# FFN gate and up: one product of 512 columns for both parts of a block, summed outside TensorE

## The chip, the cores and the metric

The kernel runs on one core of a Trainium2 chip. The metric is the device time of one execution in microseconds (us); the time of a kernel is the median of several executions. The profile is one more execution of the same program, read by the hardware profiler, with its own time.

## The reference

One layer of a decoder trunk for 256 tokens (S) of width 1024 (D), in float32. A mixer of two branches (block-sparse attention and a gated delta rule) comes first; then a feed-forward network (FFN), and then a gate on a per-layer embedding. The change lies in the FFN alone:

```python
f = rms_norm(h, ln_pre_ffn[i])
f = (jax.nn.silu(f @ w_ffn_gate[i]) * (f @ w_ffn_up[i])) @ w_ffn_down[i]
h = h + rms_norm(f, ln_post_ffn[i])
```

`w_ffn_gate` and `w_ffn_up` are 1024 x 2816, `w_ffn_down` is 2816 x 1024.

## The kernel before

Everything is kept transposed: features on the 128 partitions, the 256 tokens along the free dimension. A vector of 1024 features is 8 blocks (KB) of 128 x 256. The hidden width 2816 is 22 tiles (FT) of 128 features.

**Products in three parts.** TensorE multiplies in a type (fp32r) that holds fewer digits than float32. So each operand is split into a high part, rounded by ScalarE (ACT), and a low part, the remainder, computed by VectorE (DVE). A product is then three: high weights with the high part of the block, high weights with its low part, low weights with its high part (`mm3`, lines 242 to 244), all added up in one PSUM area. Each matmul has 256 columns and a load of 128 x 128 weights of its own.

**Weights.** `fetch` (lines 210 to 225) brings a tile of 128 x 1024 weights by DMA into `raw` (4 buffers), ACT writes `whi` (line 223), DVE, or GpSimd (POOL) for a few listed tiles, writes `wlo` (line 224). The gate and up tiles (`fg`, `fu`) share 5 buffers of each part, the down tiles (`fd`) 3. SyncE (SP) issues the DMAs in the order of use, each when a `raw` buffer is free.

**FFN.** The normed activations stand in `fh` and `fl`, eight blocks each. The first two pairs of tiles (t = 0 and 1) go through `four_tiles` (line 891), interleaved with the blocks as they get ready. From t = 2 a loop runs: for t below 22, `pair` makes the gate and the up product of tile t, both into one PSUM bank `pj` of 2 x 256 columns (24 matmuls each); `hidden` (lines 939 to 951) makes the tile's hidden values: multiply by the norm's factor `rs2` (line 941), tanh on ACT (943), the SiLU product (944), times the up half (945), then the split into `fhi` (ACT) and `flo` (DVE), line 263. In the same round `kouter` adds the down product of tile t - 2 into four PSUM banks `oacc` (24 matmuls). Two rounds at the end (t = 22, 23) hold only the down products of the last two tiles. A sum of squares over `oacc` and the rest of the layer follow.

PSUM has three banks for pairs (`bank`, tag "acc"), four for the down sums, one for statistics. `fg` and `fth`, the tiles of `hidden`, come from a pool of 4 buffers (`t1k`).

**Order.** The program is written as one stream; a scheduler sets each engine's order from it, ahead of time, so that each engine then runs a fixed list, in order, with waits on semaphores.

Of the kernel before, what the change touches and what calls it, by code (L numbers as in the profile page):

```python
# [10 lines left out]
F32R = mybir.dt.float32r  # L11
I32 = mybir.dt.int32
AF = mybir.ActivationFunctionType
ALU = mybir.AluOpType

P = 128
S = 256
D = 1024
KB = D // P
# [125 lines left out]
def layer(tc, xT, pT, wpk, wbd, vecs, cst, outT):  # L145
    nc = tc.nc
    ctx = ExitStack()

    def pool(name, bufs, st=ctx, **kw):
        p = st.enter_context(tc.tile_pool(name=name, bufs=bufs, **kw))  # L150
        return p if "space" in kw else Lines(p)
# [20 lines left out]
    def uid(s):  # L172
        count[0] += 1
        return f"{s}_{count[0]}"
# [11 lines left out]
    def t1k(name, dt=F32, pl=tmp, bufs=4):  # L186
        return pl.tile([P, S], dt, tag="t1k", bufs=bufs, name=uid(name))
# [4 lines left out]
    def bank(name):  # L192
        return ps_acc.tile([P, 2, S], F32, tag="acc", name=uid(name))
# [16 lines left out]
    def fetch(parts=1):  # L210
        i = wstate["n"]
        wstate["n"] += 1
        raw = wr.tile([P, D], F32, tag="raw", name=uid("raw_%s%d_%d" % SEQ[i]))
        pl = wstate["late"] if SEQ[i][0] in ("fg", "fu", "pg") and SEQ[i] not in EARLY else wsp
        off = VOFF if SEQ[i][0] == "va" else WOFF
        hi = pl.tile([P, D], F32R, tag="whi", off=off, room=256, name=uid("whi_%s%d_%d" % SEQ[i]))
        lo = pl.tile([P, D], F32R, tag="wlo", off=off, room=256, name=uid("wlo_%s%d_%d" % SEQ[i]))
        n = D // parts
        for c in range(0, D, n):
            cs_ = slice(c, c + n)  # L220
            nc.sync.dma_start(raw[:, cs_], wpk[i][:, cs_])
            with behind(*wstate["gate"]):
                nc.scalar.activation(hi[:, cs_], raw[:, cs_], AF.Copy)  # L223
                (nc.gpsimd if wstate["lo"](i) else nc.vector).tensor_sub(lo[:, cs_], raw[:, cs_], hi[:, cs_].bitcast(F32))  # L224
        wq[SEQ[i]] = (hi, lo)
# [4 lines left out]
    def weight():  # L230

        u = wstate["used"]
        need = max(SEQ.index(w) for w in USE[u:u + wstate["ahead"] + 1])
        while wstate["n"] <= need:
            fetch()
        wstate["used"] += 1
        return wq.pop(USE[u])
# [8 lines left out]
    endmm = [None]  # L246

    def linear(out, w, act, nk=KB, m=P):
        wh, wl = w
        for k in range(nk):  # L250
            mm3(out, wh[:, k * m:(k + 1) * m], wl[:, k * m:(k + 1) * m],
                act[0][:, k], act[1][:, k], k == 0, k == nk - 1)
            if k % 2:
                wv.tick(6 * MM)

    def pair(act):
        ps = bank("pj")
        for j in range(2):
            linear(ps[:, j], weight(), act)
        return ps  # L260

    def split_act(hi, lo, src):
        return nc.scalar.activation(hi, src, AF.Copy), nc.vector.tensor_sub(lo, src, hi.bitcast(F32))  # L263
# [37 lines left out]
    def sq_tiles(pl):  # L301
        return [pl.tile([P, S], F32, tag=f"sqacc{i}", bufs=1, name=uid("sqacc")) for i in range(2)]
# [24 lines left out]
    def stat():  # L327
        return ps_st.tile([P, S], F32, tag="st", name=uid("st"))
# [356 lines left out]
    def v_chunk(w):  # L685
        pv = bank("pv")
        for b in range(2):
            for k in range(KB):
                wh, wl = w[k // 4]
                ws = slice((k % 4) * S, (k % 4 + 1) * S)  # L690
                bs = slice(b * P, (b + 1) * P)
                nc.tensor.matmul(pv[:, b], xg[0][:, k, bs], wh[:, ws], start=k == 0, stop=False)
                nc.tensor.matmul(pv[:, b], xg[0][:, k, bs], wl[:, ws], start=False, stop=False)
                nc.tensor.matmul(pv[:, b], xg[1][:, k, bs], wh[:, ws], start=False, stop=k == KB - 1)
                if k % 2:
                    wv.tick(6 * MM)
        return pv
# [57 lines left out]
    for n, (kind, i) in enumerate(ORDER):  # L755
        if kind in ("kb", "qb"):
            ps = pair(xg)
# [7 lines left out]
        elif kind == "vb":  # L765
            ps = pair(xg)
# [4 lines left out]
        elif kind == "z":  # L771
            if yB[0] is None:
                t = mix.tile([P, 2, H, S], F32R, tag="yB", name="yBt")
                yB[0] = (t[:, 0], t[:, 1])
            ps = pair(xg)
# [5 lines left out]
        elif kind in ("ka", "qa"):  # L781
            ps = pair(xg)
# [5 lines left out]
        elif kind == "va":  # L788
            if yA[0] is None:
                t = mix.tile([P, 2, H, S], F32R, tag="dk", name="yAt")  # L790
                yA[0] = (t[:, 0], t[:, 1])
            w = [weight(), weight()]
            ps = v_chunk(w)
# [22 lines left out]
    for t in range(KB + 2):  # L816
        if t < KB:
            ps = pair(xg)
# [32 lines left out]
    fp = pool("ffn", 1)  # L851
    ft = pool("ffnt", 3)
# [4 lines left out]
    def embed(half):  # L857

        wh, wl = weight()
        got = []  # L860
        for c in range(2):
            ps = bank("pe")
            for j in range(2):
                ms = slice((2 * c + j) * 2 * P, (2 * c + j + 1) * 2 * P)
                for k in range(2):
                    mm3(ps[:, j], wh[:, ms][:, k * P:(k + 1) * P], wl[:, ms][:, k * P:(k + 1) * P],
                        ph[0][:, k], ph[1][:, k], k == 0, k == 1)
            got.append((4 * half + 2 * c, ps))
        return got
# [40 lines left out]
        rs = rsqrt_rep(ft, st, 1.0 / D, eps4, False, last)  # L910
    with behind(lastk):
        eb = embed(0)
    f = (fp.tile([P, KB, S], F32R, name="fh"), fp.tile([P, KB, S], F32R, name="fl"))
    acc = sq_tiles(ft)
    hp = tc.high_priority()
    hp.__enter__()
# [12 lines left out]
    gu, lasthi = four_tiles(f, "gu")  # L929
    wstate["ahead"] = 5  # L930
    st = stat()
    with tc.high_priority():
# [3 lines left out]
        rs2 = rsqrt_rep(ft, st, 1.0 / D, eps1, True, None, gate=True, tanh=True)  # L936
    ea2 = fp.tile([P, S], F32, name="ea2")
    nc.vector.tensor_scalar(ea2, acc[1], 4.0 * EPS, 4.0 * EPS * EPS * D / P, op0=ALU.mult, op1=ALU.add)
    def hidden(ps):
        g_ = t1k("fg", pl=ft)  # L940
        nc.vector.tensor_mul(g_, ps[:, 0], rs2)
        th = t1k("fth", pl=ft)
        nc.scalar.activation(th, g_, AF.Tanh, scale=0.5)
        nc.vector.scalar_tensor_tensor(g_, th, 1.0, g_, op0=ALU.add, op1=ALU.mult)
        nc.vector.tensor_mul(g_, g_, ps[:, 1])
        hi = ft.tile([P, S], F32R, tag="fhi", bufs=4, name=uid("fhi"))
        lo = ft.tile([P, S], F32R, tag="flo", bufs=4, name=uid("flo"))
        last = split_act(hi, lo, g_)
        if wstate["gate"]:
            wstate["gate"] = last  # L950
        return hi, lo

    with tc.high_priority():
        hid = [hidden(gu[0]), hidden(gu[1])]
    db = None
    wstate["ahead"] = 3
    for t in range(2, FT + 2):
        if t < FT:
            hid.append(hidden(pair(f)))
        if t == 5:  # L960
            stf = stat()
            nc.tensor.matmul(stf, ones, ea2, start=True, stop=False)
            embed_sq(0)
        if db is None:
            db = four()
        if t == FT + 1:
            wstate["ahead"] = 5
        lastk = kouter(db, weight(), hid[t - 2][0], hid[t - 2][1], t == 2, t == FT + 1)
        wstate["gate"] = ()
# [19 lines left out]
    pg, _ = four_tiles(h2, "pg")  # L989
# [19 lines left out]
    for m in range(4, KB):  # L1009
        ps = ps_sm.tile([P, 2, S], F32, tag="sm", name=uid("pg"))  # L1010
# [82 lines left out]
```

## Time and profile before

| | |
|---|---|
| time, median of 3 | 607.08 us (605.51 to 610.48) |
| time of the profiled execution | 605.85 us |
| its span, first to last instruction | 604.1 us |
| PE busy | 569.9 us, 94% of the span |
| PE weight loads busy | 552.1 us, 91% |
| DVE busy | 449.4 us, 74% |
| ACT busy | 320.9 us, 53% |
| mean granted TensorE clock | 0.983 of full speed |

The span is read by engine and by stretch. A matmul's own duration contains the way through the array, so the pace of matmuls is read from the distance of their starts. An idle time in brackets is that of the engine just before the instruction, with what ended it.

### The profile page before, as it was taken

How to read it: one execution, taken by the hardware profiler on the slowest of the kernel's cores; microseconds unless marked ns; L12 is line 12 of the kernel's file. 1: busy time of each engine (PE TensorE's matmuls, PEld its weight loads, DVE VectorE, ACT ScalarE, POOL GpSimd, SP SyncE). 2: the span in 40 equal slices, each digit the busy share in tenths (PEclk: the TensorE clock that was granted, in tenths of full speed). 3: DMA queues.
4: the chain of work that ended last, by engine and by line, in shares of the span. 5: the costliest groups of instructions: out<-in, count | busy, mean ns of one | idle time of the engine just before them, and what ended most of it. 6: DMA issues, size and time to landing. Idle time of an engine off the chain costs nothing.

```text
span 604.1 us, 11879 instructions
## 1 busy us (share of the span) xinstructions
PE 569.9 (94%) x4714; PEld 552.1 (91%) x4714; DVE 449.4 (74%) x891; ACT 320.9 (53%) x551; POOL 121.6 (20%) x94
## 2 busy tenths in 40 slices
PE   7798798899798899999999999899999999999997
PEld 6797697799698899999999999889999999999987
DVE  5999999864878975389566667687776666654587
ACT  6744557534357655465545555656554454444643
POOL 4234422412323446100000102420000000001250
PEclk9989988899899999999999999999999999999999
DMA  7655453732235574226666767127875655545502
GB/s 249 223 186 216 128 175 110 222 102 72 69 120 171 138 249 149 96 71 234 206 206 218 234 224 246 58 71 234 272 256 185 205 190 195 192 163 170 175 1 71
DMA packets 40631, 101.95 MB, mean 169 GB/s; under 512 B 9464, under 2 KB 16512, under 8 KB 40448
## 3 DMA queue, kind: packets, MB, share of 16 engines
q1 hardware_dynamic: 40576, 101.20, 51.0%
q8 instruction: 37, 0.61, 0.4%
q14 instruction: 18, 0.15, 0.1%
HBM read 96.70 MB, written 4.48 MB: 168 GB/s over the span
## 4 chain that ended last, share of the span: by engine, by line
PE 65%; DVE 26%; ACT 4%; issue 2%; DMA 1%; POOL 1%; SPq 0%; ACTq 0%; DVEq 0%; POOLq 0%
PE pj L242 11%; PE pj L244 11%; PE pj L243 11%; DVE cy L467 4%; PE oacc L243 4%; PE oacc L242 4%; PE oacc L244 4%; PE pp L244 2%; PE pp L242 2%; PE pp L243 2%; DVE dk L443 2%; PE pg L891 1%; PE pr L590 1%; PE py L596 1%; DVE dk L446 1%
## 5 line engine op out<-in xcount | busy, mean ns | idle before, releaser
L242 PE MATMUL oacc<-fhi,whi_fd 128*128 128x256 f32 x176 | 48.2, 277 | 1.2 <-ACT fhi L263 1.2
L243 PE MATMUL oacc<-flo,whi_fd 128*128 128x256 f32 x176 | 48.7, 278 | 0.3 <-DVE flo L263 0.3
L244 PE MATMUL oacc<-fhi,wlo_fd 128*128 128x256 f32 x176 | 48.5, 276 | 0.0
L243 PE MATMUL pj<-fl,whi_fg 128*128 128x256 f32 x160 | 44.2, 276 | 0.0
L244 PE MATMUL pj<-fh,wlo_fg 128*128 128x256 f32 x160 | 44.2, 276 | 0.0
L242 PE MATMUL pj<-fh,whi_fg 128*128 128x256 f32 x160 | 44.2, 276 | 0.0
L242 PE MATMUL pj<-fh,whi_fu 128*128 128x256 f32 x160 | 44.2, 276 | 0.0
L243 PE MATMUL pj<-fl,whi_fu 128*128 128x256 f32 x160 | 44.2, 276 | 0.0
L244 PE MATMUL pj<-fh,wlo_fu 128*128 128x256 f32 x160 | 44.2, 276 | 0.0
L224 DVE TENSOR_TENSOR wlo_fd<-raw_fd,whi_fd 128x1024 fp32r<-128x1024 f32 x22 | 27.0, 1226 | 22.6 <-ACT whi_fd L223 21.9
L224 POOL TENSOR_TENSOR wlo_pg<-raw_pg,whi_pg 128x1024 fp32r<-128x1024 f32 x4 | 8.2, 2063 | 165.4 <-ACT whi_pg L223 165.4
L223 ACT ACTIVATE whi_fd<-raw_fd 128x1024 fp32r<-128x1024 f32 x22 | 23.3, 1061 | 30.2 <-DMA raw_fd<-wpk 16.3
L223 ACT ACTIVATE whi_fg<-raw_fg 128x1024 fp32r<-128x1024 f32 x22 | 23.3, 1060 | 26.4 <-PE pj L243 19.0
L467 DVE SCALAR_TENSOR_TENSOR cy<-xr,vec,cy 128x254 f32<-128x254 f32 (+2 forms) x72 | 36.6, 547 | 0.9 <-ACT cy L465 0.7
L242 PEld LDWEIGHTS oacc<-fhi,whi_fd 128*128 128x128 f32 x176 | 32.8, 188 | 1.4 <-ACT fhi L263 1.4
L224 DVE TENSOR_TENSOR wlo_fg<-raw_fg,whi_fg 128x1024 fp32r<-128x1024 f32 x21 | 25.7, 1224 | 10.8 <-ACT whi_fg L223 10.8
L223 ACT ACTIVATE whi_fu<-raw_fu 128x1024 fp32r<-128x1024 f32 x22 | 23.3, 1058 | 19.5 <-PE pj L243 13.4
L243 PEld LDWEIGHTS oacc<-flo,whi_fd 128*128 128x128 f32 x176 | 33.0, 188 | 0.5 <-DVE flo L263 0.5
L244 PEld LDWEIGHTS oacc<-fhi,wlo_fd 128*128 128x128 f32 x176 | 33.0, 188 | 0.0
L224 DVE TENSOR_TENSOR wlo_fu<-raw_fu,whi_fu 128x1024 fp32r<-128x1024 f32 x19 | 23.3, 1224 | 12.9 <-ACT whi_fu L223 12.8
L242 PEld LDWEIGHTS pj<-fh,whi_fg 128*128 128x128 f32 x160 | 30.0, 188 | 0.0
L244 PEld LDWEIGHTS pj<-fh,wlo_fu 128*128 128x128 f32 x160 | 30.0, 188 | 0.0
(383 smaller groups left out, 2318.3 us busy)
## 6 DMA issues: line engine op xcount, KB each, us to landing
raw_fg<-wpk SPq DMA_DIRECT2D x22, 512.0 KB, 3.5
raw_fu<-wpk SPq DMA_DIRECT2D x22, 512.0 KB, 4.3
raw_fd<-wpk SPq DMA_DIRECT2D x22, 512.0 KB, 3.4
raw_qb<-wpk SPq DMA_DIRECT2D x8, 512.0 KB, 3.3
raw_ka<-wpk SPq DMA_DIRECT2D x8, 512.0 KB, 3.4
raw_qa<-wpk SPq DMA_DIRECT2D x8, 512.0 KB, 3.7
raw_vb<-wpk SPq DMA_DIRECT2D x8, 512.0 KB, 3.3
raw_va<-wpk SPq DMA_DIRECT2D x8, 512.0 KB, 3.7
```

What stands on the lines that cost most here:

```text
L223: nc.scalar.activation(hi[:, cs_], raw[:, cs_], AF.Copy)
L224: (nc.gpsimd if wstate["lo"](i) else nc.vector).tensor_sub(lo[:, cs_], raw[:, cs_], hi[:, cs_].bitcast(F32))
L242: nc.tensor.matmul(out, wh, xh, start=start, stop=False, **kw)
L243: nc.tensor.matmul(out, wh, xl, start=False, stop=False, **kw)
L244: endmm[0] = nc.tensor.matmul(out, wl, xh, start=False, stop=stop, **kw)
L443: nc.vector.scalar_tensor_tensor(dk[:, h, dst], row[:, j, b * P:(b + 1) * P], gcT[:, b, h:h + 1], mS, op0=ALU.subtract, op1=ALU.max)
L446: nc.vector.scalar_tensor_tensor(dk[:, h, dst], row[:, j, b * P:(b + 1) * P], gcT[:, b, h:h + 1], mB, op0=ALU.subtract, op1=ALU.min)
L467: nc.vector.scalar_tensor_tensor(y[:, j, sh:], xr[:, j, :S - sh], col(w + 3 - sh), y[:, j, sh:], op0=ALU.mult, op1=ALU.add)
L590: nc.tensor.matmul(pr[:, i * P:(i + 1) * P], A[:, h4[i]], Y[:, h4[i]], start=True, stop=True)
L596: nc.tensor.matmul(py[:, i * P:(i + 1) * P], X[:, i], R[:, i], start=True, stop=True)
L891: endmm[0] = nc.tensor.matmul(bk[i // 2][:, i % 2], w[:, k * P:(k + 1) * P], x[:, k], start=start and i % 2 == 0, stop=stop, skip_group_ch ...
```

## The change

`fh` and `fl` become two halves of one tile `fhl`. A new function `wide` makes one product of a weights tile: for each block the high weights meet the high and the low part side by side, 512 columns in one matmul, into a whole PSUM bank `pw` of 2 x 256 columns; the low weights meet the high part, 256 columns, added into the first half. A new function `summed` adds the halves: ACT copies the second half out of PSUM into a tile `fs`, DVE adds the first half to it. `hidden` now takes two operands: for t = 0 and 1 the PSUM areas as before, for t = 2 to 21 two `fs` tiles. A round thus has 16 matmuls per product instead of 24, two PSUM banks instead of one, two more instructions on ACT and two more on DVE.

```diff
-    f = (fp.tile([P, KB, S], F32R, name="fh"), fp.tile([P, KB, S], F32R, name="fl"))
+    fhl = fp.tile([P, 2, KB, S], F32R, name="fhl")
+    f = (fhl[:, 0], fhl[:, 1])
...
-    def hidden(ps):
+    def wide(act):
+
+        wh, wl = weight()
+        ps = bank("pw")
+        for k in range(KB):
+            nc.tensor.matmul(ps, wh[:, k * P:(k + 1) * P], act[:, :, k], start=k == 0, stop=False, skip_group_check=True)
+            endmm[0] = nc.tensor.matmul(ps[:, 0], wl[:, k * P:(k + 1) * P], act[:, 0, k], start=False, stop=k == KB - 1,
+                                        skip_group_check=True)
+        return ps
+
+    def summed(ps):
+        t = t1k("fs", pl=ft)
+        nc.scalar.activation(t, ps[:, 1], AF.Copy)
+        nc.vector.tensor_add(t, t, ps[:, 0])
+        return t
+
+    def hidden(g0, up):
         g_ = t1k("fg", pl=ft)
-        nc.vector.tensor_mul(g_, ps[:, 0], rs2)
+        nc.vector.tensor_mul(g_, g0, rs2)
...
-        nc.vector.tensor_mul(g_, g_, ps[:, 1])
+        nc.vector.tensor_mul(g_, g_, up)
...
-        hid = [hidden(gu[0]), hidden(gu[1])]
+        hid = [hidden(gu[i][:, 0], gu[i][:, 1]) for i in range(2)]
...
-            hid.append(hidden(pair(f)))
+            hid.append(hidden(*[summed(wide(fhl)) for _ in range(2)]))
```

The lines of `hidden` move: 941, 943, 944 and 945 become 958, 960, 961 and 962; the copy and the add of `summed` are lines 952 and 953.

**DVE, one round in the middle of the loop.** The names are those above; numbers behind a name tell buffers apart. Before:

```order
L941 TENSOR_TENSOR fg_5524<-pj_5463,rsr_4910 128x256
L224 TENSOR_TENSOR wlo_fg_0_892_5668<-raw_fg_0_890_5666,whi_fg_0_891_5667 128x1024
L944 SCALAR_TENSOR_TENSOR fg_5524<-fth_5526,fg_5524 128x256
L945 TENSOR_TENSOR fg_5524<-fg_5524,pj_5463 128x256
L224 TENSOR_TENSOR wlo_fd_0_902_5738<-raw_fd_0_900_5736,whi_fd_0_901_5737 128x1024
L263 TENSOR_TENSOR flo_5531<-fg_5524,fhi_5530 128x256
L224 TENSOR_TENSOR wlo_fu_0_895_5698<-raw_fu_0_893_5696,whi_fu_0_894_5697 128x1024
```

Now, the same round:

```order
L953 TENSOR_TENSOR fs_5440<-fs_5440,pw_5423 128x256
L958 TENSOR_TENSOR fg_5469<-fs_5440,rsr_4909 128x256
L224 TENSOR_TENSOR wlo_fg_0_912_5603<-raw_fg_0_910_5601,whi_fg_0_911_5602 128x1024
L953 TENSOR_TENSOR fs_5466<-fs_5466,pw_5449 128x256
L961 SCALAR_TENSOR_TENSOR fg_5469<-fth_5471,fg_5469 128x256
L962 TENSOR_TENSOR fg_5469<-fg_5469,fs_5466 128x256
L224 TENSOR_TENSOR wlo_fd_0_926_5665<-raw_fd_0_924_5663,whi_fd_0_925_5664 128x1024
L263 TENSOR_TENSOR flo_5476<-fg_5469,fhi_5475 128x256
L224 TENSOR_TENSOR wlo_fu_0_917_5629<-raw_fu_0_915_5627,whi_fu_0_916_5628 128x1024
```

One add stands ahead of the multiplication by `rs2`, the other ahead of line 961; the rest keeps its order.

**ACT, where the loop begins**, from the tanh of tiles 0 and 1 on. Before:

```order
L943 ACTIVATE fth_4924<-fg_4922 128x256
L943 ACTIVATE fth_4934<-fg_4932 128x256
L263 ACTIVATE fhi_4928<-fg_4922 128x256
L263 ACTIVATE fhi_4938<-fg_4932 128x256
L223 ACTIVATE whi_fg_0_785_4944<-raw_fg_0_784_4943 128x1024
```

Now:

```order
L960 ACTIVATE fth_4923<-fg_4921 128x256
L960 ACTIVATE fth_4933<-fg_4931 128x256
L952 ACTIVATE fs_4964<-pw_4947 128x256
L263 ACTIVATE fhi_4927<-fg_4921 128x256
L952 ACTIVATE fs_4990<-pw_4973 128x256
L263 ACTIVATE fhi_4937<-fg_4931 128x256
L223 ACTIVATE whi_fg_0_784_4942<-raw_fg_0_783_4941 128x1024
```

A copy for tile 2 stands ahead of each `fhi`.

**ACT, where the last tile's hidden values are made.** Before:

```order
L223 ACTIVATE whi_fd_0_1077_6939<-raw_fd_0_1076_6938 128x1024
L223 ACTIVATE whi_pg_0_1068_6897<-raw_pg_0_1067_6896 128x1024
L223 ACTIVATE whi_pg_0_1074_6933<-raw_pg_0_1073_6932 128x1024
L943 ACTIVATE fth_6970<-fg_6968 128x256
L263 ACTIVATE fhi_6974<-fg_6968 128x256
```

Now:

```order
L223 ACTIVATE whi_fd_0_1135_6762<-raw_fd_0_1134_6761 128x1024
L223 ACTIVATE whi_pg_0_1124_6724<-raw_pg_0_1123_6723 128x1024
L952 ACTIVATE fs_6752<-pw_6735 128x256
L223 ACTIVATE whi_pg_0_1132_6756<-raw_pg_0_1131_6755 128x1024
L952 ACTIVATE fs_6784<-pw_6767 128x256
L960 ACTIVATE fth_6789<-fg_6787 128x256
L263 ACTIVATE fhi_6793<-fg_6787 128x256
```

Both copies stand ahead of the tanh (`pg` are tiles of the stage after the FFN).

## Rows read from the trace of the kernel before

**Rows 1.** The page: busy time of each engine, and the chain that ended last.
```profile
PE 569.9 (94%) x4714; PEld 552.1 (91%) x4714; DVE 449.4 (74%) x891; ACT 320.9 (53%) x551; POOL 121.6 (20%) x94
PE 65%; DVE 26%; ACT 4%; issue 2%; DMA 1%; POOL 1%; SPq 0%; ACTq 0%; DVEq 0%; POOLq 0%
```

**Rows 2.** Windows in the loop: stretch, length, PE, PEld, DVE, ACT, POOL busy, granted clock.
```profile
440.00:480.00 40.00, 40.00 (x356) 40.00 (x355) 27.81 (x38) 19.75 (x26) 0.00 (x0) 1.00 0.65 212
520.00:560.00 40.00, 40.00 (x356) 40.00 (x355) 22.58 (x32) 16.49 (x22) 2.00 (x1) 1.00 0.52 172
```

**Rows 3.** Timeline of PE, one round: start, duration, instruction.
```profile
480.55 0.28 PE L242 MATMUL oacc<-fhi,whi_fd 128*128 128x256 f32 x1
...
483.27 0.28 PE L242 MATMUL pj<-fh,whi_fg 128*128 128x256 f32 x1
...
488.71 0.28 PE L242 MATMUL oacc<-fhi,whi_fd 128*128 128x256 f32 x1
```

**Rows 4.** Timeline of PE in the mixer: float32 products of 512, 256 and 1 columns.
```profile
67.02 1.02 PE L494 MATMUL G<-kq 128*128 128x512 f32 x2
67.88 0.59 PE L496 MATMUL G<-kq 128*128 128x256 f32 x2
68.31 0.50 PE L498 MATMUL G<-cs,qs 128*128 128x1 f32 x4
68.67 0.36 PE L242 MATMUL pj<-xhl,whi_vb 128*128 128x256 f32 x1
```

**Rows 5.** Groups of instructions on DVE and ACT, 407 to 566 us.
```profile
L224 DVE TENSOR_TENSOR wlo_fd<-raw_fd,whi_fd 128x1024 fp32r<-128x1024 f32 x21 | 25.8, 1226 | 22.6 <-ACT whi_fd L223 21.9 <-PE pj L244 0.8
L944 DVE SCALAR_TENSOR_TENSOR fg<-fth,fg 128x256 f32<-128x256 f32 x20 | 9.1, 456 | 1.0 <-ACT fth L943 1.0
L941 DVE TENSOR_TENSOR fg<-pj,rsr 128x256 f32<-128x256 f32 x20 | 8.4, 422 | 8.4 <-PE pj L244 8.3
L223 ACT ACTIVATE whi_fd<-raw_fd 128x1024 fp32r<-128x1024 f32 x21 | 22.3, 1062 | 30.2 <-DMA raw_fd<-wpk 16.3 <-PE oacc L243 11.8 <-PE oacc L244 1.4
L943 ACT ACTIVATE fth<-fg 128x256 f32<-128x256 f32 x20 | 8.0, 401 | 2.5 <-DVE fg L941 2.5
```

**Rows 6.** Timelines of ACT and DVE: three instructions in that round, one reading PSUM.
```profile
480.68 1.06 ACT L223 ACTIVATE whi_fg<-raw_fg 128x1024 fp32r<-128x1024 f32 x1 [1.71 <-PE pj L243]
...
481.78 1.23 DVE L224 TENSOR_TENSOR wlo_fg<-raw_fg,whi_fg 128x1024 fp32r<-128x1024 f32 x1 [0.61 <-ACT whi_fg L223]
...
571.35 0.38 ACT L320 ACTIVATE sq<-oacc 128x256 f32<-128x256 f32 x1
```

**Rows 7.** Timelines of ACT, PE and DVE where the loop begins.
```profile
406.06 0.42 ACT L263 ACTIVATE fhi<-fg 128x256 fp32r<-128x256 f32 x1 [0.64 <-DVE fg L945]
406.53 0.38 PE L242 MATMUL oacc<-fhi,whi_fd 128*128 128x256 f32 x1 [1.23 <-ACT fhi L263]
406.73 0.42 DVE L263 TENSOR_TENSOR flo<-fg,fhi 128x256 fp32r<-128x256 f32 x1
408.25 1.23 DVE L224 TENSOR_TENSOR wlo_fg<-raw_fg,whi_fg 128x1024 fp32r<-128x1024 f32 x1 [0.43 <-ACT whi_fg L223]
409.83 0.28 PE L242 MATMUL pj<-fh,whi_fg 128*128 128x256 f32 x1
```

**Rows 8.** Timelines of ACT, POOL, DVE and PE where the loop ends.
```profile
543.19 1.06 ACT L223 ACTIVATE whi_pg<-raw_pg 128x1024 fp32r<-128x1024 f32 x1 [0.81 <-PE pj L243]
561.47 1.06 ACT L223 ACTIVATE whi_fd<-raw_fd 128x1024 fp32r<-128x1024 f32 x1 [0.89 <-DMA raw_fd<-wpk]
563.56 4.22 POOL L224 TENSOR_TENSOR wlo_pg<-raw_pg,whi_pg 128x1024 fp32r<-128x1024 f32 x2 [17.23 <-ACT whi_pg L223]
564.34 0.40 ACT L943 ACTIVATE fth<-fg 128x256 f32<-128x256 f32 x1
564.77 1.16 DVE L944 SCALAR_TENSOR_TENSOR fg<-fth,fg 128x256 f32<-128x256 f32 x1 [0.64 <-ACT fth L943]
566.87 1.20 DVE L263 TENSOR_TENSOR flo<-fg,fhi 128x256 fp32r<-128x256 f32 x1 [0.48 <-ACT fhi L263]
568.12 0.39 PE L243 MATMUL oacc<-flo,whi_fd 128*128 128x256 f32 x1 [0.26 <-DVE flo L263]
```

## The prediction

> **What bounds the kernel now.** The page comes first: PE is busy 94% of the span and holds 65% of the chain that ended last, DVE 26% of it [rows 1]. Those are averages, so the windows inside the FFN loop come next: in 440 to 480 and in 520 to 560 us PE is busy without a gap and at full clock (granted 1.00, the 2.4 GHz level), while DVE is busy 27.8 and 22.6 us of 40 and ACT 19.8 and 16.5 [rows 2]. So from about 407 us, where the loop gets going, nearly to its end at 568 us nothing but the pace of the matmuls sets the time; a copy or an add on ACT or DVE is beside it as long as it makes nobody late. PE waits at two places only: 1.23 us at the start of the loop, for `fhi` of the first tile [rows 7], and 0.26 us at its end, for `flo` of the last [rows 8].
>
> The pace: a round holds 72 matmuls (24 down, 48 gate and up) and lasts from 480.55 to 488.71 us, 8.16 us, 113.3 ns each [rows 3]. At 2.4 GHz that is 272 cycles for 256 columns: 106.7 ns if a column takes a cycle, and 6.7 ns more. The change leaves the columns as they are (512 + 256 in place of 3 x 256); what it can save on PE is a part of those 6.7 ns.
>
> **What the products give.** Per block, three matmuls become two: 20 tiles x 2 products x 8 blocks = 320 matmuls fewer, each with its load of weights. The first of the 20 rounds ends in PE's wait for `fhi`, which is set by DVE and ACT, not by PE, so its 16 count for nothing; 304 remain. The trace has no fp32r matmul of 512 columns, so its pace is bounded from both sides. If the 6.7 ns are a price of the columns, 512 take 2 x 113.3 = 226.6 ns and nothing is saved. The rows say this is possible: the float32 products of 512 and 256 columns, which the trace shows in two passes each, take 0.86 / 2 = 430 and 0.43 / 2 = 215 ns a pass, in proportion, with next to nothing fixed [rows 4]. The other end is the same 215 ns read differently: a pass of 256 columns that lasts 516 cycles is as long a stream, beside one weight load, as 512 fp32r columns would be, and has only 2 ns on top of 213.3. Then a block takes 215 + 113.3 = 328.3 in place of 340 ns, and 304 x 11.7 ns = 3.5 us go. Between them lies a fixed price for each matmul and its load: 220 + 113.3, 304 x 6.7 ns = 2.0 us. I take 2.0: in the loop every matmul has exactly one load and one start beside it, and these are what the change makes fewer; the float32 passes read a column in two cycles and may hide them. Range 0 to 3.5. That the two halves of the 512 columns lie 8 KB apart in `fhl` has no row; if that costs, it moves toward the end of 0, and past it only if the break costs more than a second matmul does.
>
> The trace's 6.7 ns stand against the Trainium skill, "TensorE: Matmul & The Clock Gate", section "Back-to-back issue gap", which gives a matmul a fixed 2.5 ns beyond its columns; by that the saving would be 304 x 2.5 ns = 0.8 us, and the sum below would be 1.2 us higher. The same page, section "LDWEIGHTS (loading the stationary operand)", prices a load of 128 columns at 128 / 1.2 = 107 ns, by which the load and not the columns could set the pace of 113.3; the four one-column products of [rows 4] with their loads take 0.36 us, 90 ns each, so the rows don't bear that out; by the rule a block would take 213.3 + 113.3 ns, and 304 x 13.3 ns = 4.0 us would go.
>
> **What ACT and DVE get.** Forty copies on ACT, each from PSUM, 128 x 256: 0.38 us in the nearest row that reads PSUM [rows 6], 0.40 for a tanh of that size [rows 5]; 40 x 0.40 = 16 us. Forty adds on DVE with one operand in PSUM, like line 941: 0.42 us [rows 5], 40 x 0.42 = 16.8 us. What hides them is PE's round of 8.16 us, then 8.16 - 16 x 0.0067 = 8.05. DVE's round is three `wlo` of 1.23, line 944 with 0.46 and three of 0.42, 5.4 us in all; with two adds 6.2, or 77% of the round. ACT's is three `whi` of 1.06 and two of 0.40, 4.0; with two copies 4.8, or 60%.
>
> Shares don't show waits, so I walk through a round in the new order, time 0 being the end of the gate product. ACT copies at 0.1 to 0.5 and splits `fg` to 1.6; DVE adds at 0.5 to 0.9, multiplies by `rs2` to 1.3, makes `wlo_fg` to 2.8. The up product ends at 2.65; ACT copies to 3.1, does tanh to 3.5, `whi_fd` to 4.6, `fhi` to 5.0, `whi_fu` to 6.0. DVE adds at 3.15 to 3.6, goes on to 4.45 (two steps), `wlo_fd` from 4.6 to 5.8, `flo` to 6.25, `wlo_fu` to 7.5. The next gate product ends at 8.05, so about one microsecond of a round stays open.
>
> Behind the new waits stand: on ACT, behind the copy of the up half, tanh and the split of the next weights; on DVE, behind its add, the hidden values and three `wlo`. Who waits for those has time. Five buffers hold gate and up tiles: the one split from 480.68 on [rows 6] is freed when the product before ends and is met three rounds on, at 483.27 + 2 x 8.16 = 499.6 by [rows 3], over 16 us after its `wlo` ended at 483.0. A tile's hidden values are needed by the down product two rounds later. The third PSUM bank: the up product of the next round takes the bank of this round's gate product, which is free 0.9 us after that product's end and wanted 8.05 us after, so 7.1 us are open. DMAs carry the same bytes in the same order; a `raw` buffer is freed by `wlo`, which stays as often as before. Cost in the middle of the loop: 0, up to the rival below.
>
> **The two ends of the loop.** At the start ACT had 0.64 us of idle time ahead of `fhi` [rows 7], since it waited for DVE; the copy of 0.40 that now stands there fits in, as the gate product of tile 2 is long over. On DVE the first add stands ahead of `flo`, in the time in which that waited for `fhi`. What is moved is the next split: `wlo_fg` began at 408.25 and was over at 409.48, and PE's product began at 409.83 [rows 7]; with the second copy (0.40) and two adds (0.84) ahead, less the 0.43 that DVE idled there, it ends near 410.3, 0.25 us after the second matmul of that product wants it. PE's new list has a matmul of the up product in between. I put 0.1, range 0 to 0.4.
>
> At the end both copies stand ahead of the last tanh: ACT's tanh at 564.34 [rows 8] becomes 565.14, line 944's successor ends at 566.7 (1.16 us, as long as POOL runs on to 567.8), the product at 567.2, `fhi` at 567.6, `flo` from 567.67 to 568.1 without POOL or 568.9 with it. It ended at 568.07 before, when PE waited for it. So 0 to 0.8 are lost, 1.6 if copies and adds all fall in line (2 x 0.40 + 2 x 0.42). I take 0.4. What PE gains ahead of that is not lost to this chain as a whole: it starts from a split that waits for PE's product at 543 us [rows 8], with most of the gain behind it. What DMA landings hold in it (0.89 us ahead of the last `whi_fd`) moves along with it.
>
> Sum, against the profiled execution: 605.85 - 2.0 + 0.1 + 0.4 = 604.35. The median of the runs is 1.23 us above that execution; so 607.08 - 1.5 = **605.6 us**. The three runs before spread over 605.5 to 610.5, so a change below about 1% (6 us) can't be told from none.
>
> **The rivals.**
> (a) The columns set the pace: no saving, and the ends cost 0.5 us: 607.6; with both ends at their worst (0.4 + 1.6) 609.1. For it stand the proportional float32 rows; against it, that the loads fall by a third.
> (b) A matmul of 512 columns has only the 2 ns on top: 607.08 - 3.5 + 0.5 = 604.1.
> (c) Slower: PE waits for a PSUM bank. DVE idled 2.7 us of a round (8.16 less 5.4), nearly all waiting for ACT's splits and for PE's products [rows 5]. If these waits do not shrink, its round is 6.2 + 2.7 = 8.9 us against PE's 8.05: it falls 0.88 us back each round, has used up the 7.1 us of the bank after 8 rounds, and sets the other 11 of the 19 at 8.9 in place of 8.16 us: + 8.5, less 8 x 0.11 gained before, + 7.6, with the ends 615.2. It decides where DVE's waits in a round stay above 1.8 us. Against it: those waits end with PE or with ACT, which wait for PE's freed buffers (1.71 us ahead of `whi_fg` [rows 6]); that is slack that shrinks when the engine is late.
> (d) The number of columns hardly sets the pace, only the number of matmuls: 304 x 113.3 ns = 34 us less, 573. The float32 passes of 430 against 215 ns speak against it [rows 4]. The section "Back-to-back issue gap" named above has such a rule in the Trainium skill, a sustained 131 ns for 512 columns, by which 304 x 96 ns = 29 us would go; no row here agrees.
>
> **How the numbers follow.** The forecast, 604.5 to 606.9 us with small errors at the ends, has 0.60; (a) 0.19; (b) 0.13; (c) 0.06; (d) 0.02. (a), (b) and the forecast all lie within 1%. The range goes from 602.6 (case (b) with nothing lost at the ends and 1 us for the spread of runs) to 609.6 ((a) at its worst and a little of the spread); outside are (c) and (d) and the spread's rest. Faster by over 1%: (d) and a little of (b), 0.04. Slower by over 1%: (c) and a little of (a), 0.08. The rest, 0.88, is no change that can be told.
>
> **What the profile after would show.** Right: in the loop a 512-column matmul followed by one of 256 at a distance of about 220 ns, the next at 113; a round of about 8.05 us; PE without idle time between the two ends of the loop; DVE near 77% and ACT near 60% there; the last `flo` still the thing PE waits for. (a) shows 227 ns, (b) 215. (c) shows PE idle ahead of line 945 with DVE's line 953 as what ended it. The prediction would be most wrong if a strided moving operand or a shared PSUM bank made the wide matmul slower than two narrow ones, which no row here can exclude.

## The result and the profile after

The changed kernel takes 609.63 us (median of 20 runs), the kernel before 605.90 in the 20 runs beside it: a ratio of 1.0051, 95% interval 1.0034 to 1.0068. It is slower by half a per cent, where 0.25% faster was forecast; the time is also just above the range. The profiled execution took 611.85 us with a span of 610.1 and a mean granted clock of 0.978.

The page of the kernel after, its busy times and its chain, against [rows 1]:

```profile
PE 575.4 (94%) x4394; PEld 543.5 (89%) x4394; DVE 465.2 (76%) x931; ACT 332.3 (54%) x591; POOL 121.0 (20%) x94
PE 64%; DVE 25%; ACT 5%; DMA 2%; issue 2%; POOL 1%; SPq 0%; DVEq 0%; ACTq 0%; POOLq 0%
```

PE has 320 matmuls fewer and is busy 5.5 us longer; weight loads are down by 8.6 us. DVE's and ACT's 40 instructions more add 15.8 and 11.4 us. The chain is as before, mostly PE.

Of the 6.0 us between the two profiled executions, not all lies in the changed stage. The rows that bound it are the first sum of squares ahead of it, the first down product and the sum of squares behind it. Timeline of PE, first of the kernel before:

```profile
381.06 0.67 PE L325 MATMUL st<-sqacc,cs 128*128 128x256 f32 x2 [0.18 <-PE pe L243]
...
571.68 0.70 PE L325 MATMUL st<-sqacc,cs 128*128 128x256 f32 x2
```

Then of the kernel after:

```profile
383.60 0.67 PE L325 MATMUL st<-sqacc,cs 128*128 128x256 f32 x2 [0.18 <-PE pe L243]
...
409.04 0.62 PE L242 MATMUL oacc<-fhi,whi_fd 128*128 128x256 f32 x3 [0.66 <-ACT fhi L263]
...
577.65 0.70 PE L325 MATMUL st<-sqacc,cs 128*128 128x256 f32 x2
```

At 383.60 the execution is already 2.54 us late, with nothing changed so far: in its first 100 us, in the mixer, the granted clock was 0.91, before 0.95. That is not the change's. From there to the first down product it takes 25.44 us, before 25.47 (406.53 by [rows 7]). The loop, from the first down product to the sum of squares behind, takes 577.65 - 409.04 = 168.61 us, before 571.68 - 406.53 = 165.15: **3.46 us more**, which is 0.57% of the time and agrees with the ratio. All that follows is about these 3.46 us.

The windows of the loop after, columns as in [rows 2]:

```profile
440.00:480.00 40.00, 40.00 (x273) 36.82 (x272) 29.64 (x47) 21.97 (x36) 0.00 (x0) 1.00 0.61 203
520.00:560.00 40.00, 40.00 (x268) 36.63 (x267) 27.21 (x43) 19.23 (x31) 2.00 (x1) 1.00 0.52 176
```

PE is still busy without a gap and at full clock. DVE is at 74 and 68%, ACT at 55 and 48%: PE waits for neither of them, nor for a PSUM bank. So the time is in the pace of the matmuls. PE, one round:

```profile
434.75 0.28 PE L242 MATMUL oacc<-fhi,whi_fd 128*128 128x256 f32 x1
...
437.47 0.39 PE L945 MATMUL pw<-fhl,whi_fg 128*128 128x512 f32 x1
437.70 0.28 PE L946 MATMUL pw<-fhl,wlo_fg 128*128 128x256 f32 x1
437.82 0.39 PE L945 MATMUL pw<-fhl,whi_fg 128*128 128x512 f32 x1
...
443.06 0.28 PE L242 MATMUL oacc<-fhi,whi_fd 128*128 128x256 f32 x1
```

The starts are to be compared. The down product takes 437.47 - 434.75 = 2.72 us, as before (483.27 - 480.55, [rows 3]). The round takes 8.31 here, 8.32 in the mean, before 8.16: the gate and up products are 0.16 us longer in a round, 10 ns in each of their 16 blocks. A finer split of a block can't be read from rows rounded to 10 ns: a round lasts the same 8160 ns before, and 8320 after, again and again, so that the rounding falls alike in each round and doesn't average out (some numbers of the expectations below, such as 232 and 118 ns, are such means). By the starts in whole ns that the trace holds, a block before took 113.1 ns (high weights, high part), 113.0 (high, low) and 113.9 (low, high), 340 in all. Now the wide matmul takes 230.5 and the narrow one 119.3, 350 in all. The wide one is 4.4 ns slower than the two that it replaces, and the narrow one beside it 5.4 slower than it was. 19 rounds of 0.16 us are 3.04 of the 3.46 us; the rest is 0.42 at the two ends of the loop.

### The profile page after: what moved, and what is told of

It is laid out like the page before. It is cut to its first block, busy times and chain, and to the rows that moved or that the text cites. A ratio compares the mean times of both kernels' runs of the same rounds, so it can differ in the third digit from the quotient of the medians.

```text
span 610.1 us, 11332 instructions
## 1 busy us (share of the span) xinstructions
PE 575.4 (94%) x4394; PEld 543.5 (89%) x4394; DVE 465.2 (76%) x931; ACT 332.3 (54%) x591; POOL 121.0 (20%) x94
## 4 chain that ended last, share of the span: by engine, by line
PE 64%; DVE 25%; ACT 5%; DMA 2%; issue 2%; POOL 1%; SPq 0%; DVEq 0%; ACTq 0%; POOLq 0%
PE pw L945 10%; PE pj L244 6%; PE pj L242 6%; PE pj L243 6%; PE pw L946 5%; PE oacc L244 4%; PE oacc L243 4%; PE oacc L242 4%; DVE cy L467 4%; PE pp L242 2%; PE pp L244 2%; PE pp L243 2%; DVE dk L443 2%; DMA raw_fd<-wpk 2%; PE pg L891 1%
## 5 line engine op out<-in xcount | busy, mean ns | idle before, releaser
L945 PE MATMUL pw<-fhl,whi_fu 128*128 128x512 f32 x160 | 56.9, 393 | 0.0
L945 PE MATMUL pw<-fhl,whi_fg 128*128 128x512 f32 x160 | 56.9, 392 | 0.0
L946 PE MATMUL pw<-fhl,wlo_fg 128*128 128x256 f32 x160 | 45.2, 282 | 0.0
L946 PE MATMUL pw<-fhl,wlo_fu 128*128 128x256 f32 x160 | 45.1, 282 | 0.0
L945 PEld LDWEIGHTS pw<-fhl,whi_fu 128*128 128x128 f32 x160 | 30.0, 188 | 6.8
L945 PEld LDWEIGHTS pw<-fhl,whi_fg 128*128 128x128 f32 x160 | 30.1, 188 | 5.6
L946 PEld LDWEIGHTS pw<-fhl,wlo_fg 128*128 128x128 f32 x160 | 30.1, 188 | 0.1
L946 PEld LDWEIGHTS pw<-fhl,wlo_fu 128*128 128x128 f32 x160 | 30.0, 188 | 0.0
```

The source lines that it names most:

```text
L945: nc.tensor.matmul(ps, wh[:, k * P:(k + 1) * P], act[:, :, k], start=k == 0, stop=False, skip_group_check=True)
L946: endmm[0] = nc.tensor.matmul(ps[:, 0], wl[:, k * P:(k + 1) * P], act[:, 0, k], start=False, stop=k == KB - 1, skip_group_check=True)
```

## Experiments

The theories of the first runs, as the expectations number them: (1) the two halves of the 512 columns lie 8 KB apart, and the break costs; (2) the wide matmul's own pace is slower, wherever its two halves lie; (3) the new copies and adds, which read PSUM while PE writes it, slow the matmuls. Later expectations split theory 2 by where in it the price might lie, and name each version. A distance is the mean of the distances of starts in the loop, in ns of the trace, unless rows are shown; the granted clock is 1.00 there in every run (412 to 540 us). The time that a run stands beside is that of the kernel before, taken along with it.

**e1: the two parts side by side in SBUF**

```diff
-    fhl = fp.tile([P, 2, KB, S], F32R, name="fhl")
+    fhl = fp.tile([P, KB, 2, S], F32R, name="fhl")
...
-  nc.tensor.matmul(ps, wh[:, k * P:(k + 1) * P], act[:, :, k], ...
+  nc.tensor.matmul(ps, wh[:, k * P:(k + 1) * P], act[:, k], ...
```

> The tile of both parts is laid out block by block (high part of block k, then its low part), so that the 512 columns of a wide matmul are one run of addresses in place of two that lie 8 KB apart; nothing else changes. In the changed kernel a block takes 350 ns (wide matmul 232, narrow one 118), against 340 before. Theory 1 (the break in the moving operand costs): the wide matmul falls to 220 or less, a block to 333 to 340 ns, and the time falls by 3 to 5 us against the changed kernel, to 0.993 to 1.000 of the kernel before. Theory 2 (a long stream of fp32r columns beside a load of other weights costs this, wherever it lies): block 350, time 1.005 of before, as the changed kernel. Theory 3 (the copies and adds, or their reads of PSUM, slow the matmuls): block 350 as well.

Measured: 609.36 against 607.32 us beside it, ratio 1.0024 (0.9997 to 1.0051); wide 230.1 ns, narrow 119.6, round 8.32, loop 168.61 us. PE in this kernel:

```profile
438.26 0.39 PE L945 MATMUL pw<-fhl,whi_fu 128*128 128x512 f32 x1
438.50 0.28 PE L946 MATMUL pw<-fhl,wlo_fu 128*128 128x256 f32 x1
438.62 0.39 PE L945 MATMUL pw<-fhl,whi_fu 128*128 128x512 f32 x1
```

A block of 360 by these rows, which are rounded to 10 ns, and 350 in the mean: 512 adjacent columns are no faster than 256 and 256 with 8 KB between them. Theory 1 falls. The ratio can't be told from that of the change; the loop is the same to 0.01 us.

**e2: the sums stay, the wide matmul is two narrow ones again**

```diff
-  nc.tensor.matmul(ps, wh[:, k * P:(k + 1) * P], act[:, :, k], ...
+  for j in range(2):
+      nc.tensor.matmul(ps[:, j], wh[:, k * P:(k + 1) * P], act[:, j, k], ...
```

> The wide matmul is written as two of 256 columns again, the high part into the first half of the bank and the low part into the second; copies, adds and the two banks a round stay. Theories 1 and 2: three matmuls in 340 ns a block as before, time 0.999 to 1.002 of before (only the end of the loop loses 0.4 us). Theory 3 (copies, adds or PSUM): a block of 347 to 350 ns, time 1.004 to 1.006 of before.

Measured: 608.15 against 607.32 us, ratio 1.0029 (1.0002 to 1.0056); round 8.16, loop 166.91 us. PE in this kernel (a row may hold two matmuls that follow each other):

```profile
437.98 0.39 PE L946 MATMUL pw<-fhl,whi_fu 128*128 128x256 f32 x2
...
438.32 0.39 PE L946 MATMUL pw<-fhl,whi_fu 128*128 128x256 f32 x2
438.54 0.28 PE L948 MATMUL pw<-fhl,wlo_fu 128*128 128x256 f32 x1
438.66 0.28 PE L242 MATMUL oacc<-fhi,whi_fd 128*128 128x256 f32 x1
```

340 ns a block (437.98, 438.32, 438.66), with every copy and every add in place. Theory 3 falls: the round is back at 8.16 and only the width of the matmul was undone. What is left, 1.76 us more than before where 0.4 was expected, lies at the two ends. At the head the second down block starts 0.43 us later after the first than before (9.17 against 8.74) and lasts 3.02 in place of 2.72, 0.73 in all; the rest, about 1.0, is the tail:

```profile
560.11 1.06 ACT L223 ACTIVATE whi_fd<-raw_fd 128x1024 fp32r<-128x1024 f32 x1 [0.58 <-DMA raw_fd<-wpk]
561.06 0.28 PE L242 MATMUL oacc<-fhi,whi_fd 128*128 128x256 f32 x1
562.42 0.42 DVE L955 TENSOR_TENSOR fs<-fs,pw 128x256 f32<-128x256 f32 x1
562.88 1.69 DVE L960 TENSOR_TENSOR fg<-fs,rsr 128x256 f32<-128x256 f32 x1
567.67 0.38 PE L242 MATMUL oacc<-fhi,whi_fd 128*128 128x256 f32 x1 [1.01 <-ACT fhi L263]
```

PE waits 1.01 us for `fhi` of the last tile; before it waited 0.26 for `flo` [rows 8]. The last tile's chain begins behind `whi_fd` and `wlo_fd`, that is behind a DMA, so the first add stands 562.42 - 561.06 = 1.36 us behind the start of the down block. In the changed kernel PE is later at this place, the add stands only 568.45 - 567.87 = 0.58 behind the same block, and the wait is 0.23: the 0.78 us of difference is exactly what PE waits less. So the sums cost 1.76 us where PE keeps its pace of before; in the changed kernel the slower rounds cover a part of it.

**e3: the wide matmul stays, the sums are left out** (the hidden values are made from the first half alone)

```diff
-    hid.append(hidden(*[summed(wide(fhl)) for _ in range(2)]))
+    hid.append(hidden(*[wide(fhl)[:, 0] for _ in range(2)]))
```

> The wide matmuls stay, but nothing copies or adds the second half: the hidden values are made from the first half alone, so the product of the high weights with the low part is left out of the result. Theories 1 and 2: block 350 ns, round 8.31 us as in the changed kernel. Theory 3: block 333 to 340 ns.

Measured: 608.72 us in one execution; round 8.32, wide 230.2 ns, narrow 119.5, loop 167.51 us; PE doesn't wait at the tail. Without one copy or add the matmuls are as slow as with them. This is the counterpart of e2: the width by itself costs 2.36 us of loop (3.04 by the pace, less 0.68 at the ends), the sums by themselves 1.76, both together 3.46. On top of the width, then, the sums cost 1.10 us.

**e4: all eight wide matmuls first, then all eight narrow ones**

```diff
   for k in range(KB):
       nc.tensor.matmul(ps, wh[:, k * P:(k + 1) * P], act[:, :, k], ...
+  for k in range(KB):
       endmm[0] = nc.tensor.matmul(ps[:, 0], wl[:, k * P:(k + 1) * P], act[:, 0, k], ...
```

> In each product the eight wide matmuls come first, then the eight narrow ones, so that a wide matmul is followed by a load of the next high weights and not of low ones. Theory 1 (break): the wide matmul keeps 232 ns or near it, a block stays 345 to 352 ns. Theory 2 in the form that the change between high and low weights costs: wide 218 to 225, narrow 107 to 113, block 330 to 340. Theory 3: block 350.

Measured: 608.47 us in one execution; round 8.29 to 8.30. PE in this kernel:

```profile
438.81 1.09 PE L947 MATMUL pw<-fhl,wlo_fu 128*128 128x256 f32 x8
439.74 0.28 PE L242 MATMUL oacc<-fhi,whi_fd 128*128 128x256 f32 x1
...
442.46 2.02 PE L945 MATMUL pw<-fhl,whi_fg 128*128 128x512 f32 x8
444.32 0.86 PE L947 MATMUL pw<-fhl,wlo_fg 128*128 128x256 f32 x6
```

Eight wide matmuls take 444.32 - 442.46 = 1.86 us, 232.5 ns each; eight narrow ones 439.74 - 438.81 = 0.93, 116 each. The wide one is as slow among its like as beside a narrow one, and the narrow ones are slower than the 113.3 of before even among their like: it isn't the alternation.

**e5: another place of the gate and up weights in their buffers**, at an offset of 0, and of 24, in place of 88

```diff
-  off = VOFF if SEQ[i][0] == "va" else WOFF
+  off = VOFF if SEQ[i][0] == "va" else 0 if SEQ[i][0] in ("fg", "fu") else WOFF
```

> The changed kernel with the gate and up weights (both parts) at offset 0 within their buffers in place of 88 bytes; the offset was chosen with matmuls of 256 columns. Theory 2a (the stream of fp32r columns and the load of weights beside it get in each other's way in the on-chip memory, depending on their addresses): the wide matmul moves by at least 3 ns from 232, in either direction, and with it the round of 8.32 us by at least 0.05 us. Theory 2b (512 columns of fp32r take 232 ns by themselves): 232 ns, round 8.30 to 8.34 us.

> The same with offset 24 (88 less 64). Theory 2a: if the addresses count modulo 64 bytes, as offset 88 (232 ns, 8.32 us a round); if they count in larger units, another value. Theory 2b: 232 ns, round 8.30 to 8.34 us.

Measured, one execution each, beside 612.04 us: offset 0, 613.42 us, round 8.39, wide 236 ns, narrow 117; offset 24, 607.99 us, round 8.28 to 8.29, wide 233, narrow 114. So a block takes 353, 347 or 350 ns at offsets of 0, 24 and 88. At offset 0 the wide matmul moves by more than the 3 ns of theory 2a: the place of the weights does move the pace, by a few ns. But none of the three comes down to the 340 of before.

**e6: half the load beside the wide matmul** (the narrow matmul has 64 columns of weights: half the rows of its part of the sum are left out)

```diff
-  endmm[0] = nc.tensor.matmul(ps[:, 0], wl[:, k * P:(k + 1) * P], act[:, 0, k], ...
+  endmm[0] = nc.tensor.matmul(ps[:64, 0], wl[:, k * P:k * P + 64], act[:, 0, k], ...
```

> The narrow matmul takes only the first 64 columns of the low weights, so that the load that runs beside the wide matmul has half its columns; the low weights' part of the other 64 features is left out of the result. Theory 2a: the 19 ns that the wide matmul takes beyond 213 shrink by half, to 222 to 224 ns, and a round gets 0.14 us shorter or more. Theory 2b: the wide matmul stays at 232 ns, the round at 8.32 us; at most the narrow one changes.

Measured: 610.17 us in one execution, beside 612.04; round 8.29 to 8.30. PE in this kernel:

```profile
446.66 0.39 PE L945 MATMUL pw<-fhl,whi_fg 128*128 128x512 f32 x1
446.89 0.28 PE L946 MATMUL pw<-fhl,wlo_fg 128*64 128x256 f32 x1
447.01 0.39 PE L945 MATMUL pw<-fhl,whi_fg 128*128 128x512 f32 x1
```

Wide 230.3 ns, as with the full load to within 1 ns: what is loaded while the wide matmul runs doesn't set its pace. The load that runs beside the narrow one, of the next high weights, is still a full one. The Trainium skill, "TensorE: Matmul & The Clock Gate", section "LDWEIGHTS (loading the stationary operand)", makes a load's price proportional to its columns, an estimated 107 ns for 128; the load halved here, hidden either way, shows that such a price isn't in these 230 ns.

**e7: the wide matmul reads only the upper two bytes of each number** (as bf16; the lower digits of both operands are left out), the narrow one as before

```diff
-  nc.tensor.matmul(ps, wh[:, k * P:(k + 1) * P], act[:, :, k], ...
+  nc.tensor.matmul(ps, wh.bitcast(mybir.dt.bfloat16)[:, 2 * k * P + 1:2 * (k + 1) * P:2],
+                   act[:, :, k].bitcast(mybir.dt.bfloat16)[:, :, 1::2], ...
```

> The wide matmul reads only the upper two bytes of each number, weights and block (as bf16 at a step of 4 bytes); the lower digits are left out of the result. Same columns, same addresses, same loads in number. Theory 2a: with half the bytes the wide matmul falls to 213 to 220 ns, the round to 8.1 us or less. Theory 2b in the form that the type fp32r costs: the same. Theory 2c (any matmul of 512 columns beside a 128-column load takes 232 ns): 232 ns, round 8.32 us.

Measured: 611.73 us in one execution, beside 612.04; round 8.51 to 8.54. PE in this kernel:

```profile
446.76 0.40 PE L945 MATMUL pw<-fhl,whi_fu 128*128 128x512 bf16 x1
446.80 0.48 PE L947 MATMUL pw<-fhl,wlo_fu 128*128 128x256 f32 x1
447.12 0.40 PE L945 MATMUL pw<-fhl,whi_fu 128*128 128x512 bf16 x1
```

Starts of 41 and 320 ns apart, 361 a block: where types alternate, the records no longer part one matmul from the next, and the change of type has a price of its own. This run tells nothing about bytes; e9 was made for that.

**e8: fewer columns in the wide matmul** (448, 384, 320 of the 512, on top of e1 and e3: the rest of the low part and the sums are left out)

```diff
-  nc.tensor.matmul(ps, wh[:, k * P:(k + 1) * P], act[:, k], ...
+  nc.tensor.matmul(ps.rearrange("p a b -> p (a b)")[:, :448], wh[:, k * P:(k + 1) * P],
+                   act[:, k].rearrange("p a b -> p (a b)")[:, :448], ...
```

> The wide matmul of the block-by-block layout takes 448 columns: the 256 of the high part and the first 192 of the low part; what the other columns would give is left out, and so are the copies and adds (the hidden values are made from the first half, as in the run without sums, which kept the pace). So only the number of columns changes; with 512 the wide matmul takes 231.5 ns. Theory 2d (fp32r columns come at a price each, somewhat over a cycle, with a small credit for each matmul; a line through 113 ns at 256 and 231.5 at 512): 202 ns. Theory 2e (a fixed 6.7 ns up to some number of columns, and a further fixed price past it): 193 ns if the price is not due yet, 205 if it is.

> The same with 384 columns (256 of the high part, 128 of the low part). Theory 2d: 172 ns. Theory 2e: 167 ns if the further price is not due yet, 178 if it is.

> The same with 320 columns (256 of the high part, 64 of the low part). Theory 2d: 143 ns. Theory 2e: 140 ns if the further price is not due yet, 152 if it is.

Measured, beside 606.31 us:

| columns | time, us | round, us | wide, ns | ns per column | narrow, ns |
|---|---|---|---|---|---|
| 512 (e1, with sums) | 609.36 (beside 607.32) | 8.32 | 230.1 | 0.449 | 119.6 |
| 448 | 600.52 | 7.86 to 7.92 | 202.8 | 0.453 | 116.9 |
| 384 | 591.02 | 7.41 | 174.7 | 0.455 | 118.3 |
| 320 | 582.11 | 6.97 | 146.1 | 0.457 | 118.0 |

PE in the kernels of 448, 384 and 320 columns, in this order:

```profile
442.70 0.36 PE L945 MATMUL pw<-fhl,whi_fg 128*128 128x448 f32 x1
442.90 0.28 PE L947 MATMUL pw<-fhl,wlo_fg 128*128 128x256 f32 x1
```

```profile
442.67 0.34 PE L945 MATMUL pw<-fhl,whi_fu 128*128 128x384 f32 x1
442.84 0.28 PE L947 MATMUL pw<-fhl,wlo_fu 128*128 128x256 f32 x1
```

```profile
444.29 0.31 PE L945 MATMUL pw<-fhl,whi_fg 128*128 128x320 f32 x1
444.44 0.28 PE L947 MATMUL pw<-fhl,wlo_fg 128*128 128x256 f32 x1
```

The time grows with the columns, but not in proportion to them. A straight line through the four has 0.438 ns per column (a cycle at 2.4 GHz is 0.417) and 6.4 ns fixed. For 256 columns this line gives 118.4, which is near the narrow matmuls of the same kernels (116.9 to 119.6) and 5 ns above those of the kernel before (113.3). The forecast's form, a cycle a column plus a fixed 6.7, would give 140.0, 166.7, 193.4 and 220.0: it falls short by 6.1, 8.0, 9.4 and 10.1 ns, a gap that grows with the columns, and for the narrow matmul by 4 to 6. So a fixed price of the forecast's size fits these runs; what the forecast lacks is a price of some 0.02 ns a column above a cycle, and the narrow matmuls of before, with 6.7 ns above their columns, have no room for both. Of the versions in the expectations 2d (202, 172 and 143 ns) is the nearest, low by 1 to 3 ns; 2e with the further price due (205, 178 and 152) is high by 2 to 6. The Trainium skill, "TensorE: Matmul & The Clock Gate", section "Back-to-back issue gap", gives a matmul by itself a cycle a column and a fixed 2.5 ns, by estimate 215.8 ns for 512 columns; the 230.1 measured here lie above that.

**e9: both matmuls read the upper two bytes alone** (the edit of e7 for the narrow one, too)

> Both matmuls of a block, the wide and the narrow one, read only the upper two bytes of each number as bf16 (the lower digits are left out of the result), so that no type changes between them; columns, addresses and copies and adds are those of the changed kernel. Theory 2d in the form that the four bytes of an fp32r column set the price: wide 213 to 219 ns, narrow 107 to 112, a round near 8.0 us. If any 512 columns beside a load cost it: 232 and a round of 8.3 us.

Measured: 608.59 us in one execution, beside 606.31; round 8.18. PE in this kernel:

```profile
440.19 0.39 PE L945 MATMUL pw<-fhl,whi_fu 128*128 128x512 bf16 x1
440.42 0.28 PE L947 MATMUL pw<-fhl,wlo_fu 128*128 128x256 bf16 x1
440.53 0.39 PE L945 MATMUL pw<-fhl,whi_fu 128*128 128x512 bf16 x1
```

Wide 226.5 ns, narrow 114.6: 4 and 5 ns less than in the changed kernel, 341 a block, far from the 213.3 of one cycle a column. Halving what the type holds, at the same stride of 4 bytes, doesn't halve what a block takes above a cycle a column (320 ns): it falls from 30 to 21 ns. That the bytes read set it, one form of 2d, isn't confirmed by this; a packed bf16 operand was not tried.

## Why the prediction was wrong

**What bounds the kernel: right.** PE has no gap between the ends of the loop in either kernel, and a slower pace of the matmuls went into the time whole.

**What the products give: this step failed.** It took the 6.7 ns that a narrow matmul lasts beyond a cycle a column for a price of the matmul and its load alone. So it put a block at 220 + 113.3 ns, and 304 starts fewer at 2.0 us back. Measured are 230.5 + 119.3: both matmuls of a block are slower than forecast. The term is 19 x 0.16 = + 3.0 us, 5.0 from the forecast, which is all of the error and a little more. e2 and e3 show that this comes with the width alone. A fixed price of about the forecast's size may well be there (6.4 ns by the line of e8); but by the same line the columns of a block with a wide matmul cost more than a cycle each, 0.438 in place of 0.417 ns, and that outweighs what a start less gives back.

**The bound of 0 was wrong, too.** Rival (a), the columns set the pace, comes nearest, with a saving of nothing, 607.6. But it charged 512 columns with twice the 113.3 ns of 256, and left the narrow matmul as it was; the block is 10 ns slower than that. The trace had no fp32r matmul of 512 columns, so neither end of the bracket could show what a wide one adds; the prediction named this itself ("a strided moving operand or a shared PSUM bank") as what would make it most wrong. The stride is excluded by e1. The bank isn't the reason either as far as e2 goes: there the two halves of one bank are written by two narrow matmuls, at 340 ns a block.

Two readings of [rows 4] misled. The float32 passes are in proportion, but at two cycles a column and 2 ns more (430 and 215 ns), without the price that fp32r has here; they could not tell what 512 columns of fp32r take. And the four one-column products don't take 90 ns each. Only the second starts sooner, 28 ns behind the first; from then on the starts are 112, 111 and 112 ns apart. The last two and the start behind them:

```profile
68.45 0.36 PE L498 MATMUL G<-cs,qs 128*128 128x1 f32 x2
68.67 0.36 PE L242 MATMUL pj<-xhl,whi_vb 128*128 128x256 f32 x1
```

So with a load of 128 columns even a product of a single column comes only every 111 or 112 ns, and the rows do allow that the load, not the columns, sets the 113.3 ns of a narrow matmul. No run tests this: e6 halves the load beside the wide matmul only. It would not explain the result, since by it the wide matmul would take little more than its 213.3 ns.

The prediction also took 113.3 ns for the price of 256 columns as such. The same trace has slower ones at full clock, in the mixer:

```profile
80.13 0.28 PE L694 MATMUL pv<-whi_va,xhl 128*128 128x256 f32 x1
...
84.45 0.29 PE L694 MATMUL pv<-whi_va,xhl 128*128 128x256 f32 x1
```

These are 36 starts apart: 4.32 us, 120 ns each. Something other than the number of columns moves the pace of a narrow matmul by 7 ns, without any wide one near.

What stays open is why a block with a wide matmul takes 350 ns and one of three narrow ones 340, at the same 768 columns. It isn't the copies and adds (e2, e3), the break of 8 KB (e1), the alternation (e4) or the load beside the wide matmul (e6). The place of the weights shifts it by up to 6 ns a block (e5), the type by 9 (e9, 341 a block); neither was followed further, and other places of the activations were not tried. So the place of the operands in memory, together with the width, is a rival that stands untested.

**The ends of the loop: right in sum, by luck.** Forecast + 0.5, measured 0.42. The rows of the tail after:

```profile
567.87 0.28 PE L242 MATMUL oacc<-fhi,whi_fd 128*128 128x256 f32 x1
568.22 4.23 POOL L224 TENSOR_TENSOR wlo_pg<-raw_pg,whi_pg 128x1024 fp32r<-128x1024 f32 x2 [16.58 <-ACT whi_pg L223]
568.45 0.42 DVE L953 TENSOR_TENSOR fs<-fs,pw 128x256 f32<-128x256 f32 x1
568.90 1.69 DVE L958 TENSOR_TENSOR fg<-fs,rsr 128x256 f32<-128x256 f32 x1
570.52 0.41 DVE L953 TENSOR_TENSOR fs<-fs,pw 128x256 f32<-128x256 f32 x1
571.14 1.59 DVE L961 SCALAR_TENSOR_TENSOR fg<-fth,fg 128x256 f32<-128x256 f32 x1 [0.21 <-ACT fth L960]
573.70 0.38 PE L242 MATMUL oacc<-fhi,whi_fd 128*128 128x256 f32 x1 [0.23 <-ACT fhi L263]
```

The chain of the last tile is longer than walked through, because line 958 now takes 1.69 us beside POOL; PE waits for `fhi`, not for `flo`. It waits no longer than before only because PE itself comes later. At the head the scheduler also moved two matmuls of a statistic (`st<-ea,cs`) from behind the first down matmuls into PE's wait for `fhi`; the section on the change and the prediction have nothing of this. e2, where they stand as before, has the price without either cover: 0.73 at the head, above the bound of 0.4, and about 1.0 at the tail, within the bound of 1.6.

**The middle of the loop: right.** Cost 0, no wait for a PSUM bank: rival (c), DVE's round of 8.9 us, didn't come (its price was also added up wrongly: 11 rounds of 8.9 in place of 8.16 us are 8.1, not 8.5). The groups on DVE and ACT between 409 and 573 us, columns as in [rows 5]:

```profile
L953 DVE TENSOR_TENSOR fs<-fs,pw 128x256 f32<-128x256 f32 x40 | 16.6, 414 | 2.4 <-ACT fs L952 2.4
L958 DVE TENSOR_TENSOR fg<-fs,rsr 128x256 f32<-128x256 f32 x20 | 10.9, 545 | 0.5
...
L952 ACT ACTIVATE fs<-pw 128x256 f32<-128x256 f32 x39 | 14.3, 366 | 2.0 <-PE pw L946 2.0
```

Adds of 0.414 and copies of 0.366 us are the forecast's 0.42 and 0.40. The 40 adds wait 2.4 us in all, and DVE's waits did shrink, as the prediction held against (c). Rival (d), the number of matmuls sets the pace, is far off: a 512-column matmul takes 230 ns, not 113.

By its pace no run that keeps all columns beats the kernel before: the best block with a wide matmul takes 347 ns (e5; 341 with digits left out, e9), and the sums cost 1.1 to 1.8 us on top.

## What to carry to other kernels

Before matmuls are merged, measure the wide one in the block in which it will stand, with its neighbours, by the distance of starts: here both it and the matmul beside it got slower, and that ate the starts saved. A bound that is taken from rows of one width says nothing about another; leave room on both sides of it. Read distances in the trace's finest unit; in a loop that repeats exactly, rounded rows mislead however many are averaged. And a stage that hides extra work on other engines in its middle still pays for it at its two ends, where one tile's chain is all that is left: 1.8 us here for 40 copies and 40 adds (e2), 1.1 where the matmuls had become slower (e3 against the changed kernel).

## What the runs showed of the hardware

- Matmuls of fp32r at a granted clock of 1.00, each with a load of 128 columns: 146.1, 174.7, 202.8 and 230.1 ns for 320, 384, 448 and 512 columns, each followed by one of 256 with 117 to 120 ns (e8, e1). With no wide one in the block 256 columns take 113.3 ns in the FFN loop and 120 in a stage of the mixer.
- A float32 product of one column with a load of 128 columns starts 111 to 112 ns after the one ahead of it (kernel before, 68.3 to 68.7 us).
- Alternating bf16 and fp32r from one matmul to the next gave 361 ns a block, 11 more than fp32r alone, although the wide matmul had half the bytes (e7).
- DVE's operations whose operands all stand in SBUF took 1.69 (line 958) and 1.59 us (line 961) while POOL ran its two `wlo_pg` (568.22 to 572.45), against means of 0.42 and 0.46 for lines 941 and 944 before [rows 5]; the adds with an operand in PSUM 0.41 in the same stretch (rows of the tail above). Before, the multiplication by `rs2` read PSUM. So moving an operand from PSUM to SBUF made this step four times as long while POOL was at work; this kernel has little of that in its loop.
- The place of the weights in their buffers moved a block between 347 and 353 ns (e5).
